# Experts in a new order: gathers of 256 slots, an early ranking, and biases of thin sets in one product

## The chip, the cores and the metric

One NeuronCore of a Trainium2 chip runs the whole program. The metric is the device time of one execution in microseconds, as the median of several runs. The engines are TensorE (PE for products, PEld for the loads of their stationary side), VectorE (DVE), ScalarE (ACT), GpSimd (POOL) and SyncE (SP). SP issues the transfers of weights here.

## The reference

Two blocks act on 512 tokens of width 1024, in fp32. The first has a mixer and then a mixture of experts (MoE); the second has two attention layers. The change lies in the MoE:

```python
logits = xt @ router_w + router_b
top_vals, top_idx = lax.top_k(logits, 4)          # 32 experts, 4 for each token
gates = softmax(top_vals)
# for each expert e, for the tokens that chose it:
hu = xb @ w_up[e] + b_up[e]                       # 1024 -> 2048
g, lin = minimum(hu[:, :1024], 7), clip(hu[:, 1024:], -7, 7)
y = ((lin + 1) * g * sigmoid(1.702 * g)) @ w_down[e] + b_down[e]
# summed over a token's experts, each times its gate
```

## The kernel before, in words

**Ranks and sets.** The router counts the tokens of each expert, and `moe_order` ranks the experts by count, the largest first (expert 0 stays first). It works with a handful of products and small vector operations, and leaves `self.order` (the expert of each rank, which SP reads into a register to address weights), `self.perm` (a one-hot matrix), `self.selr` (selectors for bias rows) and ranked copies of slots and gates (`Rp`, `tokp`). Ranks 0 to 17 have a *wide* set of 128 slots, ranks 18 to 31 a *thin* set of 64; rank 1 has a wide and a thin set. A rank is a *unit*.

**Precision.** Wide sets work with fp32r products. Every operand is split into a high and a low part, and three products stand for one. `moe_split` splits a half piece of weights: ScalarE makes the high part, VectorE the low part, into four pairs of buffers (`wh`/`wl` three, `sph`/`spl` one). Thin sets work with fp32 products on the raw weights, in two column halves of the array at once (64 slots each), and need no split. A thin set's raw buffer is held until TensorE is done with it; a wide set's until VectorE has split it.

**Weights.** Each expert has twelve pieces of 1 MB: four for each half of the up product, four for the down product. `load_piece` puts them into six raw buffers in turn (two `w`, four `w2`), so SP can be six pieces ahead. SP issues them in the order of their use: next unit's first half, last unit's down product, this unit's second half.

**A unit's work on TensorE** (`moe`): first half of the up product (`expert_up(0)`), in the middle of which the last unit's result is transposed (`mid`); then the last unit's down product (`moe_down`), whose rows GpSimd scatters into the residual in DRAM by an indirect transfer; in the last unit of a group, the gather of the next group; then the second half (`expert_up(1)`). The scheduler of the framework may move instructions of different strands past each other.

**Gathers.** `slot_sets` gathers the tokens of a *group* of units. It makes a one-hot matrix (`eoh`) on VectorE and multiplies: 8 chunks x 4 token tiles x 2 parts, 64 products, with as many columns as the group has slots. ScalarE takes the result from four banks of PSUM into `xT` (wide, split) or `xN` (thin). `moe_groups` writes the groups by hand: `[W]`, then pairs `[W T]` of 192 slots, rank 1 alone (192), one group `[W W]` of 256, more pairs: 17 groups.

**Biases.** `ebias` holds the bias rows of all experts, high and low parts. The last product of a group adds the expert's row: for a wide set one fp32r product of 512 columns with a selector column (`sel`), for a thin set two fp32 products, one for each column half (L1290, two records each).

Of the kernel before, what the change touches and what calls it, by code (L numbers as in the profile page):

```python
# [20 lines left out]
P = 128  # L21
# [41 lines left out]
for _n, _w in (("ident", 128), ("ones", 128), ("cmask", 128), ("smask", 128), ("cmpm", 4 * 32), ("cmpv", 4),  # L63
               ("invf", 32), ("hm", 4), ("hh", 2), ("lt", 128), ("gmask", 128), ("iota1", 128), ("iotap", 1),
               ("rst", S), ("lte", 128), ("selc", 32), ("lom", 1), ("dump", 1), ("ndd", 1), ("dn2", 1),
               ("keyb", 32), ("keyp", 1), ("cap", 1), ("avg", 4 * 64)):
    CST.add(_n, _w)
# [19 lines left out]
class Kern:  # L87
# [1006 lines left out]

    def moe_order(self):

# [6 lines left out]
        nc.tensor.matmul(ps[:, 0:NE], self.C["ones"], cnt.rearrange("p a e -> p (a e)"), start=True, stop=True)  # L1103
        nc.tensor.matmul(ps[:, NE:NE + 1], n4.rearrange("p a e -> p (a e)"), self.C["ones"][:, 0:1], start=True, stop=True)
        kb, self.perm = (self.t([P, NE], tag=f"ord{n}", bufs=1) for n in range(2))
        cc, kp, rank = (self.t([P, 1], tag=f"orc{n}", bufs=1) for n in range(3))
# [4 lines left out]
        nc.vector.tensor_reduce(rank, kb, axis=AXX, op=OP.add)  # L1111
        nc.vector.tensor_scalar(self.perm, self.C["iota1"][:, 0:NE], rank, None, op0=OP.is_equal)
        pe = self.perm[0:NE]
        ps = self.psum("tr")
        nc.tensor.matmul(ps[0:1, 0:NE], self.C["iotap"][0:NE], pe, start=True, stop=True)
        nc.tensor.matmul(ps[0:NE, NE:NE + 1], pe, cc[0:NE], start=True, stop=True)
        nc.tensor.matmul(ps[0:NE, NE + 1:NE + 2], pe, self.C["iotap"][0:NE], start=True, stop=True)
        self.order = self.t([1, NE], I32, tag="ori", bufs=1)
        nc.vector.tensor_copy(self.order, ps[0:1, 0:NE])

        self.cco = self.t([NE, 2], tag="cco", bufs=1)
        nc.vector.tensor_copy(self.cco, ps[0:NE, NE:NE + 2])
        for half in range(2):
            nc.gpsimd.tensor_scalar(self.selr[:, half, 1:NE], self.perm[:, 1:NE], self.C["hh"][:, half:half + 1], None,
                                    op0=OP.mult)
        bd = self.t([P, NT, NE], tag="orb", bufs=1)
        nc.vector.tensor_tensor(bd, self.perm[:, None, :].to_broadcast([P, NT, NE]),
# [4 lines left out]
        for n, v in enumerate(src):  # L1132
            nc.tensor.transpose(pt[:, n * P:(n + 1) * P], flat(v), self.ident)
        xt = self.t([P, 3 * P], tag="ort", bufs=1)
        nc.scalar.copy(xt, pt[:, 0:3 * P])
# [31 lines left out]

    def slot_sets(self, sets):


        nc = self.nc
        n = sum(self.width(kind) for kind, *_ in sets)
        oh = self.t([P, NT, 2 * C], F32R, tag="eoh", bufs=1)[:, :, 0:n]
        xs, at, o = [], [], 0
        for kind, R, *_ in sets:
            w = self.width(kind)
            sh = [P, NT, w]
            nc.vector.tensor_tensor(oh[:, :, o:o + w], self.C["iota1"][:, None, 0:w].to_broadcast(sh),
                                    R[:, :, None].to_broadcast(sh), op=OP.is_equal)
            if kind == "wide":  # L1180
                xs.append(self.t([P, 2, KC, C], F32R, tag="xT", bufs=2))
            else:
                xs.append(self.t([P, KC, CN], tag="xN", bufs=2))
            at.append(slice(o, o + w))
            o += w
        for k0, bank in zip(range(0, KC, 2), ("tr", "tr", "o", "o2")):
            pt = self.psum(bank)
            for q in range(2):
                k = k0 + q
                for t in range(NT):  # L1190
                    for m, r in enumerate(self.rows):
                        nc.tensor.matmul(pt[:, q * n:(q + 1) * n], r[:, t, k * P:(k + 1) * P], oh[:, t],  # L1192
                                         start=(t == m == 0), stop=(t == NT - 1 and m == 1))
            for (kind, *_), x, a in zip(sets, xs, at):
                f = self.t([P, 2, C], tag="ef", bufs=2) if kind == "wide" else x[:, k0:k0 + 2, :]
                for q in range(2):
                    k = k0 + q
                    nc.scalar.activation(f[:, q], pt[:, q * n + a.start:q * n + a.stop], AF.Identity,
                                         scale=self.s2[:, k:k + 1], bias=self.b2[:, k:k + 1])
                if kind == "wide":  # L1200
                    hi, lo = (x[:, m, k0:k0 + 2, :] for m in range(2))
                    nc.scalar.activation(hi, f, AF.Copy)
                    nc.vector.tensor_tensor(lo, f, hi, op=OP.subtract)
# [64 lines left out]
    def expert_mm(self, xT, pieces, ps, bias=None, ready=()):  # L1268

        nc = self.nc  # L1270
        xh, xl = xT
        for m, half in enumerate(self.half_pieces(pieces)):
            wh, wl = ready[m] if m < len(ready) else self.moe_split(*half)
            for q in range(2):
# [3 lines left out]
                nc.tensor.matmul(ps, xh[:, k, :], wl[:, q, :], start=False, stop=(k == KC - 1 and not bias))  # L1278
        if bias:
            nc.tensor.matmul(ps, *bias, start=False, stop=True)  # L1280

    def thin_mm(self, x, pieces, ps, bias=None):


        nc = self.nc
        ws = [(n, w.rearrange("p (k f) -> p k f", k=4)) for n, w in pieces]
        jobs = [(x[:, 4 * (n % 2) + q, :], w[:, q, :]) for n, w in ws for q in range(4)] + ([bias] if bias else [])
        for n, (a, w) in enumerate(jobs):
            for c in range(2):
                nc.tensor.matmul(ps[CN * c:CN * (c + 1), 0:256], a, w[:, c * 256:(c + 1) * 256], start=(n == 0),  # L1290
                                 stop=(n == len(jobs) - 1))

    def expert_up(self, half, sets, pieces, pos, mid=None, selr=None):
# [3 lines left out]
        selr = self.selr if selr is None else selr  # L1297
        sel = selr[:, half, pos:pos + 1]
        out = []
        for m, bank in enumerate(("mm", "s")):  # L1300
            row = self.ebias[:, m * 512:(m + 1) * 512]
            two = pieces[2 * m:2 * m + 2]

            for kind, x, _ in sorted(sets, key=lambda v: v[0]):
                ps = self.psum(bank)
                out.append((kind, ps))
                if kind == "wide":
                    self.expert_mm([x[:, n] for n in range(2)], two, ps, (sel.to_broadcast([P, P]), row))
                else:
                    self.thin_mm(x, two, ps, (sel.bitcast(F32).to_broadcast([P, CN]), row.bitcast(F32)))  # L1310
            if mid and not m:
# [65 lines left out]
    def moe_bias(self):  # L1377
# [5 lines left out]
        for m in range(4):  # L1383
            c0 = m // 2 * D
            nc.sync.dma_start(raw[32 * m:32 * m + 32], self.A["exp_b"][:, c0:c0 + D])
        yield
# [3 lines left out]
    @staticmethod  # L1390
    def moe_groups():


        wide = lambda n: (n, [("wide", 0)])
        thin = lambda n: (n, [("thin", 0)])
        pairs = [[wide(n + 2), thin(NF + n)] for n in range(NE - NF)]
        rest = [wide(n) for n in range(NE - NF + 2, NF)]
        rest = [rest[n:n + 2] for n in range(0, len(rest), 2)]
        both = [[(1, [("wide", 0), ("thin", C)])]]
        return [[wide(0)]] + pairs[:3] + both + pairs[3:6] + rest + pairs[6:]  # L1400

    def moe(self, xin):
# [11 lines left out]

        def make(g, R, tok):

            sets = []
            for pos, kinds in g:
                for kind, first in kinds:
# [5 lines left out]
                    sets.append((kind, r, tok[:, :, pos, :], dsts[:, n:n + 1], gates[:, n:n + 1]))  # L1425
            xs, index = self.slot_sets(sets)
            xs = iter(xs)
# [8 lines left out]
        for half in range(2):  # L1436
            nc.gpsimd.tensor_scalar(self.selr[:, half, 0:1], self.C["selc"][:, 0:1], self.C["hh"][:, half:half + 1], None,
                                    op0=OP.mult)
        self.g2n = self.t([P, 512], tag="g2n", bufs=1)
        for half in range(2):  # L1440
            r = slice(64 * half, 64 * half + 64)
            nc.gpsimd.tensor_copy(self.g2n[r], self.g2b[r, 512 * half:512 * half + 512])
        w = load(0, range(4))
        xs, index = make(groups[0], self.R, self.tok)
        index()
# [4 lines left out]
        for n, (pos, kinds) in enumerate(units):  # L1450
# [7 lines left out]
            if not n:  # L1458
                self.moe_order()
            if prev:  # L1460
# [54 lines left out]
    def job(self, selr):  # L1515
# [25 lines left out]
        for half in range(2):  # L1541
            nc.vector.tensor_tensor(selr[:, half], s1, self.C["hh"][:, half:half + 1], op=OP.mult)
        m = self.t([P, NT, NE], tag="orb", bufs=1)
        sel3 = selb[:, None, :].to_broadcast([P, NT, NE])
# [667 lines left out]
def const_array():  # L2212
# [35 lines left out]
    put("keyp", key[p % NE][:, None])  # L2248
    put("cap", np.array(CAP, np.float32)[p % NE][:, None])
    put("hh", np.where(p[:, None] // 64 == np.arange(2)[None, :], 1.0, 0.0))  # L2250
    put("hm", np.where(p[:, None] // 32 == np.arange(4)[None, :], 1.0, 0.0))
# [77 lines left out]
```

## Time and profile before

| | us |
|---|---|
| median of 3 runs | 2686.78 (2685.45 to 2688.61) |
| profiled execution | 2686.94 |
| its span, first to last instruction | 2685.1 |
| TensorE busy with products | 2561.9 (95%) |
| VectorE busy | 1796.4 (67%) |
| ScalarE busy | 1275.6 (48%) |
| MB moved, mean GB/s | 566.77, 211 |

The mixer takes the first 395 us, the MoE stands from there to about 1580 us, and the second block fills the rest. Starts of TensorE's products are read from the timeline; their ends are modelled, so the price of a product is read from start to start.

### The profile page before, as it was taken

Reading aid. Unit: us, or ns where it says so; the run is one execution under the profiler, and the core shown is the slowest. Engines: PE = TensorE matmul, PEld = TensorE weight load, DVE = VectorE, ACT = ScalarE, POOL = GpSimd, SP = SyncE. Lnnn points to the kernel's source line nnn. Section 1 sums busy time; section 2 is a strip of 40 time slices with the busy share of each in tenths; the row PEclk is TensorE's granted clock in tenths of the full one; section 3 lists DMA queues with packets and bytes.
Section 4 is the critical chain, followed back from the end, with each engine's and each line's share of the span. In section 5 each row is a group of like instructions: output and inputs, shape, how many; then the busy total and the mean of one; then the engine's idle time right before and its main releaser. Section 6 shows DMA issues by size and latency. Waiting matters only on the chain.

```text
span 2685.1 us, 40235 instructions
## 1 busy us (share of the span) xinstructions
PE 2561.9 (95%) x15431; PEld 2003.9 (75%) x15431; DVE 1796.4 (67%) x3400; ACT 1275.6 (48%) x2202; POOL 159.9 (6%) x151
## 2 busy tenths in 40 slices
PE   5998879999999999999999969989999999999998
PEld 5875678777777778777777757776777887767778
DVE  6886667666666688666666645596775656877764
ACT  3443546545555566444455534444444433534443
POOL 1001010100000000000000010011001000100001
PEclk9998788999999999999999989999999999999999
DMA  7531236999699999999999952221112521311124
GB/s 283 203 120 65 77 134 254 367 376 367 228 359 376 380 363 344 383 379 376 380 376 384 378 192 79 67 93 66 46 48 79 189 95 49 111 63 48 33 84 151
DMA packets 85828, 566.77 MB, mean 211 GB/s; under 512 B 9984, under 2 KB 10576, under 8 KB 22144
## 3 DMA queue, kind: packets, MB, share of 16 engines
q1 hardware_dynamic: 76368, 536.55, 51.5%
q0 software_dynamic: 7968, 24.16, 3.9%
q10 hardware_dynamic: 1296, 3.44, 0.3%
q8 instruction: 123, 2.02, 0.3%
q14 instruction: 73, 0.60, 0.1%
HBM read 543.93 MB, written 20.19 MB: 210 GB/s over the span
## 4 chain that ended last, share of the span: by engine, by line
PE 72%; DVE 6%; DMA 2%; ACT 2%; issue 2%; POOL 1%; ACTq 0%; DVEq 0%; SPq 0%; POOLq 0%
PE mm L396 5%; PE mm L397 5%; PE mm L398 5%; PE mm L1290 4%; PE s L1290 4%; PE o L1290 4%; PE o L1278 3%; PE mm L1276 3%; PE mm L1278 2%; PE o L1276 2%; PE o L1277 2%; PE s L1276 2%; PE mm L1277 2%; PE s L1278 2%; PE s L1277 2%; PE o L1192 2%
## 5 line engine op out<-in xcount | busy, mean ns | idle before, releaser
L1260 ACT ACTIVATE wh<-w 128x1024 fp32r<-128x1024 f32 x324 | 337.5, 1060 | 286.2 <-DMA w<-w_exp 131.7
L1261 DVE TENSOR_TENSOR wl<-w,wh 128x1024 fp32r<-128x1024 f32 x324 | 388.2, 1221 | 84.8 <-ACT wh L1260 84.0
L215 DVE TENSOR_TENSOR wl<-w,wh 128x1024 fp32r<-128x1024 f32 x194 | 237.0, 1223 | 176.3 <-ACT wh L214 175.1
L214 ACT ACTIVATE wh<-w 128x1024 fp32r<-128x1024 f32 x194 | 204.8, 1059 | 234.6 <-PE mm L397 97.9
L372 PE MATMUL mm<-wl,aTh 128*128 128x256 f32 x816 | 238.1, 293 | 5.6 <-DVE wl L215 5.6
L371 PE MATMUL mm<-wh,aTh 128*128 128x256 f32 x816 | 238.7, 294 | 2.2 <-ACT wh L214 1.3
L373 PE MATMUL mm<-wh,aTl 128*128 128x256 f32 x816 | 238.1, 293 | 0.8 <-DVE aTl L309 0.8
L396 PE MATMUL mm<-aTh,wh 128*128 128x512 f32 x560 | 228.3, 408 | 0.0
L397 PE MATMUL mm<-aTl,wh 128*128 128x512 f32 x560 | 225.5, 403 | 0.0
L398 PE MATMUL mm<-aTh,wl 128*128 128x512 f32 x560 | 224.9, 402 | 0.0
L372 PEld LDWEIGHTS mm<-wl,aTh 128*128 128x128 f32 x816 | 161.0, 197 | 9.4 <-DVE wl L215 6.3
L371 PEld LDWEIGHTS mm<-wh,aTh 128*128 128x128 f32 x816 | 160.4, 197 | 6.6 <-ACT wh L214 1.9
L373 PEld LDWEIGHTS mm<-wh,aTl 128*128 128x128 f32 x816 | 160.7, 197 | 4.5 <-issue 3.1
L464 ACT ACTIVATE P<-s,smx 128x256 f32<-128x256 f32 (+3 forms) x176 | 92.7, 528 | 86.8 <-DVE smx L461 85.7
L1261 DVE TENSOR_TENSOR spl<-w,sph 128x1024 fp32r<-128x1024 f32 x108 | 132.1, 1223 | 1.2 <-ACT sph L1260 1.2
L1260 ACT ACTIVATE sph<-w 128x1024 fp32r<-128x1024 f32 x108 | 114.2, 1057 | 26.5 <-PE mm L1277 10.3
L396 PEld LDWEIGHTS mm<-aTh,wh 128*128 128x128 f32 x560 | 106.3, 190 | 24.1 <-issue 4.9
L398 PEld LDWEIGHTS mm<-aTh,wl 128*128 128x128 f32 x560 | 106.3, 190 | 23.8 <-issue 3.0
L397 PEld LDWEIGHTS mm<-aTl,wh 128*128 128x128 f32 x560 | 105.8, 189 | 23.2 <-issue 3.8
L1319 DVE TENSOR_SCALAR eg<-s 128x512 f32<-128x512 f32 (+1 forms) x66 | 37.6, 569 | 111.6 <-PE s L1280 71.6
L1290 PE MATMUL mm<-w,xN 128*64 128x256 f32 x960 | 110.2, 382 | 0.0
L1290 PE MATMUL s<-w,xN 128*64 128x256 f32 x960 | 109.5, 381 | 0.0
(617 smaller groups left out, 6073.7 us busy)
## 6 DMA issues: line engine op xcount, KB each, us to landing
w<-w_exp SPq DMA_DIRECT2D x384, 1024.0 KB, 8.9
w<-w_in SPq DMA_DIRECT2D x57, 1024.0 KB, 4.8
w<-w_out SPq DMA_DIRECT2D x24, 1024.0 KB, 4.9
w<-ada_w SPq DMA_DIRECT2D x19, 1024.0 KB, 4.9
w<-cmp_w SPq DMA_DIRECT2D x8, 1024.0 KB, 4.8
w<-w_up SPq DMA_DIRECT2D x16, 512.0 KB, 3.3
xm<-hd POOLq DMA_DIRECT2D x5, 512.0 KB, 3.6
aTl<-ada_w SPq DMA_DIRECT2D x2, 1024.0 KB, 7.8
```

Source lines behind the costliest of these rows:

```text
L214: self.nc.scalar.activation(hi, src, AF.Copy)
L215: (self.nc.gpsimd if pool else self.nc.vector).tensor_tensor(lo, src, hi, op=OP.subtract)
L371: nc.tensor.matmul(v[:, q, :], ah[k][:, ts], w_h, start=(k == 0), stop=False)
L372: nc.tensor.matmul(v[:, q, :], ah[k][:, ts], w_l, start=False, stop=False)
L373: nc.tensor.matmul(v[:, q, :], al[k][:, ts], w_h, start=False, stop=(k == kk - 1))
L396: nc.tensor.matmul(ps, w_h, ah[k], start=(k == 0), stop=False)
L397: nc.tensor.matmul(ps, w_h, al[k], start=False, stop=False)
L398: nc.tensor.matmul(ps, w_l, ah[k], start=False, stop=(k == kk - 1))
L1260: nc.scalar.activation(hi, w, AF.Copy)
L1261: (nc.gpsimd if n in self.LO_POOL else nc.vector).tensor_tensor(lo, w, hi, op=OP.subtract)
L1276: nc.tensor.matmul(ps, xh[:, k, :], wh[:, q, :], start=(k == 0), stop=False)
L1290: nc.tensor.matmul(ps[CN * c:CN * (c + 1), 0:256], a, w[:, c * 256:(c + 1) * 256], start=(n == 0), stop=(n == len(jobs) - 1))
```

## The change

The groups have up to 256 slots: `[W T T]` or `[W W]` in a row written out by hand, 14 groups in place of 17; the thin ranks are taken from the smallest up. `moe_order` becomes a generator, `order_ranks`, which is run in steps from inside the first gather; its rest runs where the whole stood before. A thin set's bias is added by one fp32r product over the whole array, first in its group of products, with a selector matrix `selt` that GpSimd makes for each thin set; `ebias` is laid out for it, so that a wide set adds its bias in two products of 256 columns. A third buffer for `xN`, a constant `hcol` and two shared tags come with it.

```diff
-    def moe_order(self):
+    def order_ranks(self):
...
         nc.tensor.matmul(ps[:, NE:NE + 1], n4.rearrange("p a e -> p (a e)"), self.C["ones"][:, 0:1], start=True, stop=True)
+        yield
...
         nc.vector.tensor_scalar(self.perm, self.C["iota1"][:, 0:NE], rank, None, op0=OP.is_equal)
+        yield
         pe = self.perm[0:NE]
-        ps = self.psum("tr")
+        ps = self.psum("s")
...
         nc.vector.tensor_copy(self.order, ps[0:1, 0:NE])
+        yield
...
+        self.sele = self.perm
...
-    def slot_sets(self, sets):
+    def slot_sets(self, sets, mid=iter(())):
         nc = self.nc
+        next(mid, None)
...
-                xs.append(self.t([P, KC, CN], tag="xN", bufs=2))
+                xs.append(self.t([P, KC, CN], tag="xN", bufs=3))
...
+        next(mid, None)
         for k0, bank in zip(range(0, KC, 2), ("tr", "tr", "o", "o2")):
...
+            if k0 == 2:
+                next(mid, None)
...
-        if bias:
-            nc.tensor.matmul(ps, *bias, start=False, stop=True)
+        for c in range(2 if bias else 0):
+            nc.tensor.matmul(ps[:, c * 256:(c + 1) * 256], bias[0][:, c:c + 1].to_broadcast([P, P]), bias[1], start=False,
+                             stop=(c == 1))
...
-        jobs = [(x[:, 4 * (n % 2) + q, :], w[:, q, :]) for n, w in ws for q in range(4)] + ([bias] if bias else [])
+        if bias:
+            nc.tensor.matmul(ps[:, 0:256], *bias, start=True, stop=False)
+        jobs = [(x[:, 4 * (n % 2) + q, :], w[:, q, :]) for n, w in ws for q in range(4)]
...
+        if any(kind == "thin" for kind, *_ in sets) and not half:
+            self.selt = self.t([P, P], F32R, tag="selt", bufs=2)
+            nc.gpsimd.tensor_scalar(self.selt, self.hcol, self.sele[:, pos:pos + 1], None, op0=OP.mult)
...
-            c0 = m // 2 * D
-            nc.sync.dma_start(raw[32 * m:32 * m + 32], self.A["exp_b"][:, c0:c0 + D])
+            src = self.A["exp_b"][:, 0:2 * D].rearrange("e (g c j) -> e g c j", g=4, c=2)[:, :, m // 2]
+            nc.sync.dma_start(raw[32 * m:32 * m + 32].rearrange("p (g j) -> p g j", g=4), src)
...
-        pairs = [[wide(n + 2), thin(NF + n)] for n in range(NE - NF)]
-        rest = [wide(n) for n in range(NE - NF + 2, NF)]
-        rest = [rest[n:n + 2] for n in range(0, len(rest), 2)]
-        both = [[(1, [("wide", 0), ("thin", C)])]]
-        return [[wide(0)]] + pairs[:3] + both + pairs[3:6] + rest + pairs[6:]
+        w = [wide(n) for n in range(2, NF)][::-1]
+        t = [(n, [("thin", 0)]) for n in range(NF, NE)]
+        both = (1, [("wide", 0), ("thin", C)])
+        sizes = "3232313232313"
+        out = [[wide(0)]]
+        for n, c in enumerate(sizes):
+            if c == "3":
+                out.append([w.pop(), t.pop(), t.pop()])
+            elif c == "2":
+                out.append([w.pop(), w.pop()])
+            else:
+                out.append([both if n < 6 else w.pop()])
+        return out
...
+        nc.gpsimd.dma_start(self.hcol, self.A["cst"][:, o:o + n])
...
-        xs, index = make(groups[0], self.R, self.tok)
+        order = self.order_ranks()
+        xs, index = make(groups[0], self.R, self.tok, order)
...
             if not n:
-                self.moe_order()
+                for _ in order:
+                    pass
```

## Rows read from the trace of the kernel before

**Rows 1.** The page's span in 40 equal slices, busy tenths: TensorE, transfers.

```profile
PE   5998879999999999999999969989999999999998
...
DMA  7531236999699999999999952221112521311124
```

**Rows 2.** Stage windows: length, busy us of each engine, granted clock, DMA share, GB/s.

```profile
413.00:1557.00 1144.00, 1134.41 (x7281) 869.51 (x7280) 755.17 (x1015) 606.98 (x886) 68.98 (x34) 1.00 0.92 357
...
1170.06:1238.70 68.64, 68.04 (x455) 51.91 (x453) 43.24 (x58) 34.50 (x53) 3.84 (x2) 1.00 0.96 376
...
1238.70:1250.52 11.82, 11.82 (x53) 9.32 (x51) 8.63 (x9) 5.41 (x6) 2.29 (x1) 1.00 0.99 373
...
1219.36:1231.64 12.28, 12.28 (x59) 9.72 (x55) 7.56 (x14) 5.42 (x7) 0.00 (x0) 1.00 1.01 424
...
952.99:1045.47 92.48, 91.36 (x444) 74.15 (x442) 83.63 (x94) 66.11 (x81) 6.86 (x3) 1.00 0.94 350
...
420.00:440.00 20.00, 20.00 (x103) 16.41 (x102) 18.75 (x38) 11.16 (x13) 1.75 (x2) 1.00 0.26 100
```

**Rows 3.** Waits of TensorE's products, 390 to 1580 us: total us, times, longest.

```profile
PE o L1278 <- DVE wl L1261: 5.5, 10, 0.6
PE tr L1192 <- DVE vc L1499: 4.9, 1, 4.9
```

**Rows 4.** Transfer queue of the scatters, 1170 to 1239 us: packets, MB, share.

```profile
q0 software_dynamic: 288, 0.79, 6.0%
```

**Rows 5.** Chain that ended last: start, us, engine and line.

```profile
398.64 7.06 PE tr L1192 x32
...
1231.71 7.06 PE o L1290 x64
```

**Rows 6.** Stage windows of the gather products (L1192) alone: PE, PEld, clock.

```profile
398.64:1557.49 1158.85, 139.89 (x1088) 137.27 (x1088) 0.99 0.92 357
...
919.80:923.20 3.40, 3.40 (x29) 3.29 (x28) 1.00 0.93 325
1206.73:1210.29 3.56, 3.56 (x34) 3.51 (x32) 1.00 1.02 350
...
398.64:412.33 13.69, 13.69 (x64) 13.69 (x64) 0.50 0.96 368
```

**Rows 7.** Timeline of TensorE: start, us, line, out<-in, shape, records.

```profile
1210.34 3.67 PE L1290 MATMUL mm<-w,xN 128*64 128x256 f32 x32
1213.85 0.60 PE L1290 MATMUL mm<-ebias,selr 128*64 128x256 f32 x4
1214.28 3.62 PE L1290 MATMUL s<-w,xN 128*64 128x256 f32 x32
1217.73 0.60 PE L1290 MATMUL s<-ebias,selr 128*64 128x256 f32 x4
1218.26 0.61 PE L1217 MATMUL tr<-orT,eoh 128*128 128x4 f32 x4
...
1250.20 0.39 PE L1280 MATMUL s<-ebias,selr 128*128 128x512 f32 x1
1250.52 0.44 PE L1290 MATMUL mm<-w,xN 128*64 128x256 f32 x2
```

**Rows 8.** Weight loads (L209), 1170 to 1239 us: from issue to landing.

```profile
DMA to landing us min/median/max: 4.7/9.4/13.1
```

**Rows 9.** Waits of TensorE's products, 925 to 965 us.

```profile
PE mm L1278 <- DVE wl L1261: 1.6, 2, 1.1
```

**Rows 10.** Waits of SP, 400 to 440 us.

```profile
SPq L209 <- DVE orc L1111: 29.9, 1, 29.9
```

**Rows 11.** Timeline of GpSimd, 395 to 600 us.

```profile
401.15 0.29 POOL L1101 COPY rn<-before 128x128 f32<-128x128 f32 x1
...
433.76 1.75 POOL L1124 TENSOR_SCALAR selr<-ord,cstcmask 128x31 fp32r<-128x31 f32 x2 [31.96 <-DVE ord L1112]
...
576.15 1.55 POOL L1374 DMA_INDIRECT xm<-ey,eix  x1 [32.58 <-DVE ey L1366]
```

More of the change, by code (lines that the diff above doesn't have):

```diff
@@ L65 @@
                ("rst", S), ("lte", 128), ("selc", 32), ("lom", 1), ("dump", 1), ("ndd", 1), ("dn2", 1),
-               ("keyb", 32), ("keyp", 1), ("cap", 1), ("avg", 4 * 64)):
+               ("keyb", 32), ("keyp", 1), ("cap", 1), ("avg", 4 * 64), ("hcol", 128)):
     CST.add(_n, _w)
@@ L1125, in moe_order @@
                                     op0=OP.mult)
-        bd = self.t([P, NT, NE], tag="orb", bufs=1)
+        bd = self.t([P, NT, NE], tag="eg1", bufs=1)
         nc.vector.tensor_tensor(bd, self.perm[:, None, :].to_broadcast([P, NT, NE]),
@@ L1133, in moe_order @@
             nc.tensor.transpose(pt[:, n * P:(n + 1) * P], flat(v), self.ident)
-        xt = self.t([P, 3 * P], tag="ort", bufs=1)
+        xt = self.t([P, 3 * P], tag="eg0", bufs=1)
         nc.scalar.copy(xt, pt[:, 0:3 * P])
@@ L1286, in thin_mm @@
         ws = [(n, w.rearrange("p (k f) -> p k f", k=4)) for n, w in pieces]
-        jobs = [(x[:, 4 * (n % 2) + q, :], w[:, q, :]) for n, w in ws for q in range(4)] + ([bias] if bias else [])
+        if bias:
+            nc.tensor.matmul(ps[:, 0:256], *bias, start=True, stop=False)
+        jobs = [(x[:, 4 * (n % 2) + q, :], w[:, q, :]) for n, w in ws for q in range(4)]
         for n, (a, w) in enumerate(jobs):
             for c in range(2):
-                nc.tensor.matmul(ps[CN * c:CN * (c + 1), 0:256], a, w[:, c * 256:(c + 1) * 256], start=(n == 0),
+                nc.tensor.matmul(ps[CN * c:CN * (c + 1), 0:256], a, w[:, c * 256:(c + 1) * 256], start=(n == 0 and not bias),
                                  stop=(n == len(jobs) - 1))
@@ L1297, in expert_up @@
         selr = self.selr if selr is None else selr
-        sel = selr[:, half, pos:pos + 1]
+        sel = selr[:, :, pos]
+        if any(kind == "thin" for kind, *_ in sets) and not half:
+            self.selt = self.t([P, P], F32R, tag="selt", bufs=2)
+            nc.gpsimd.tensor_scalar(self.selt, self.hcol, self.sele[:, pos:pos + 1], None, op0=OP.mult)
         out = []
         for m, bank in enumerate(("mm", "s")):
-            row = self.ebias[:, m * 512:(m + 1) * 512]
+            row = self.ebias[:, (2 * half + m) * 256:(2 * half + m + 1) * 256]
             two = pieces[2 * m:2 * m + 2]
@@ L1307, in expert_up @@
                 if kind == "wide":
-                    self.expert_mm([x[:, n] for n in range(2)], two, ps, (sel.to_broadcast([P, P]), row))
+                    self.expert_mm([x[:, n] for n in range(2)], two, ps, (sel, row))
                 else:
-                    self.thin_mm(x, two, ps, (sel.bitcast(F32).to_broadcast([P, CN]), row.bitcast(F32)))
+                    self.thin_mm(x, two, ps, (self.selt, row))
             if mid and not m:
@@ L1394, in moe_groups @@
         wide = lambda n: (n, [("wide", 0)])
-        thin = lambda n: (n, [("thin", 0)])
-        pairs = [[wide(n + 2), thin(NF + n)] for n in range(NE - NF)]
-        rest = [wide(n) for n in range(NE - NF + 2, NF)]
-        rest = [rest[n:n + 2] for n in range(0, len(rest), 2)]
-        both = [[(1, [("wide", 0), ("thin", C)])]]
-        return [[wide(0)]] + pairs[:3] + both + pairs[3:6] + rest + pairs[6:]
+        w = [wide(n) for n in range(2, NF)][::-1]
[11 more added lines that the diff above has]
+        return out
     def moe(self, xin):
@@ L1413, in moe, with make @@
         cols = {}
-        def make(g, R, tok):
+        def make(g, R, tok, mid=iter(())):
             sets = []
@@ L1425, in make @@
                     sets.append((kind, r, tok[:, :, pos, :], dsts[:, n:n + 1], gates[:, n:n + 1]))
-            xs, index = self.slot_sets(sets)
+            xs, index = self.slot_sets(sets, mid)
             xs = iter(xs)
@@ L1438, in moe @@
                                     op0=OP.mult)
+        self.hcol = self.t([P, P], tag="hcol", bufs=1)
+        o, n = CST.at["hcol"]
+        nc.gpsimd.dma_start(self.hcol, self.A["cst"][:, o:o + n])
         self.g2n = self.t([P, 512], tag="g2n", bufs=1)
@@ L1542, in job @@
             nc.vector.tensor_tensor(selr[:, half], s1, self.C["hh"][:, half:half + 1], op=OP.mult)
-        m = self.t([P, NT, NE], tag="orb", bufs=1)
+        m = self.t([P, NT, NE], tag="eg1", bufs=1)
         sel3 = selb[:, None, :].to_broadcast([P, NT, NE])
@@ L2249, in const_array @@
     put("cap", np.array(CAP, np.float32)[p % NE][:, None])
+    put("hcol", np.where(p[:, None] // 64 == np.arange(P)[None, :] // 64, 1.0, 0.0))
     put("hh", np.where(p[:, None] // 64 == np.arange(2)[None, :], 1.0, 0.0))
```

## The prediction

> **What bounds the kernel now.** I read the page's forty slices first. In slices 7 to 22, the expert phase, TensorE is busy nine tenths or more, and the transfers are nearly as full [rows 1]. Two resources compete there, so the next question is which of them the other waits for.
>
> The stage windows say TensorE. From 413 to 1557 us it is busy 1134.41 of 1144.00 us at the full clock, and one steady pair of a wide and a thin unit takes 68.64 us with 68.04 busy [rows 2]. The waits agree: over the whole phase the products wait 5.5 us in total for the split's low part and 4.9 us once at the first gather, and nothing else is longer [rows 3]. So time taken off TensorE in this phase comes off the end, as long as the weights keep arriving.
>
> They have little to spare. In a full stretch the queue moves 424 GB/s, so a piece of 1.0486 MB takes 2.48 us [rows 2]. A pair needs 24 pieces, 59.5 us, and its two scatters take 6.0% of the engines for about the pair's time, 4.1 us (wide 2.7, thin 1.4, by their sizes): 63.6 us of transfers against 68.64 us of TensorE [rows 2, 4]. The margin is 5 us a pair on average, and an average hides the order. A half of a wide unit gives TensorE 11.82 us for four pieces, which is 9.9 us of transfers; the down product of a thin unit gives 7.06 us for the same four [rows 2, 5]. Wide units refill the six raw buffers, thin units drain them.
>
> **Gathers.** Before there are 17: one of 128 slots, 15 of 192, one of 256, each 64 products whatever the width. After there are 14: two of 128, one of 192, eleven of 256. The columns in sum stay the same, so everything hangs on what a product costs by width. 29 products of 256 columns fill 3.40 us, 0.117 us each; of 192 columns 32 start in 3.56 us, 0.111 each; the first gather's 64 of 128 take 13.69 us at a granted clock of 0.50 (1.2 GHz), 0.214 each, hence 0.107 at twice that [rows 6]. The width is almost free. At those spacings the late gathers cost 15 x 7.10 + 7.49 = 114.0 us before and 11 x 7.49 + 7.10 + 6.85 = 96.3 after: 17.7 saved. All gathers together are busy 139.89 us [rows 6], so with their interruptions the 16 late ones average (139.89 - 13.69) / 16 = 7.9 us; if the interruptions go too, the saving nears 21. I take 19, with 17.7 and 21 as ends.
>
> **Thin biases.** A thin set has four bias steps, each of four records (two fp32 products, one for each column half). Starts give the price. The step at 1213.85 takes 0.43 us when thin products follow; the one at 1217.73 takes 0.53 when work 128 wide follows [rows 7]. Leaving the thin shape costs 0.10. Entering it costs 0.08: a wide bias ahead of thin work takes 0.32 us [rows 7], one of the 50 products that fill a wide half 11.82 / 50 = 0.24 [rows 2]. Before, a set pays 3 x 0.53 + 0.43 + 3 x 0.08 = 2.26 us. After, each step is one fp32r product of 256 columns on the whole array; the nearest row is the gather's, 0.117 [rows 6]. But it stands inside thin work, so every block goes from 128 wide to thin and back: 0.12 + 0.08 + 0.10 = 0.30, 1.2 us a set. Saved 1.06 a set, 16 us for 15 sets. Bounds: with no price for shapes 2.02 - 0.48 = 1.54 a set, 23 us; if the new product costs as much as a thin step with both changes (0.61), nothing. It has the gather product's shape, so nothing is too low an end; I keep 5 and 23.
>
> The Trainium skill, TensorEngine Tiling (Array Packing), Key Properties, says that changing the tiling mode drains the array, and gives no figure. The 0.43 against 0.53 us agrees. Without a drain this edit would be worth 23 us, with it 16.
>
> **Wide biases.** One product of 512 columns becomes two of 256: 2 x 0.117 against 0.24 [rows 2, 6]. I cost it at nothing.
>
> **Weights for two thin units in a row.** The new order is W, WTT, WW, WTT, WW, WTT, the unit with both kinds, WTT, WW, WTT, WW, WTT, W, WTT. Seven times two thin units stand together; before they never did. From the start of the first thin unit to the end of its down product TensorE needs 2 x (3.51 + 0.30) = 7.6, a wide down product of 11.3 (the 11.82 half without its biases), 7.6, 7.6 for the second unit's first half, and 7.06: 41.2 us [rows 2, 5, 7]. Those 20 pieces take 49.6 us and a wide scatter 2.7: 52.3. The shortage is 11 us. What can cover it is five raw buffers ahead, 12.4 us, less what a landing takes beyond its own 2.48 us (the shortest landing is 4.7): 10.2 [rows 8]. So each double thin stands on the edge. I take 1 us for each, 7 in all; ends 0 and 21. The one after the unit with both kinds has a single wide unit ahead instead of three: 2 us more. The last has no gather behind it: its remaining 7.6 + 7.06 = 14.7 us meet 8 pieces and a scatter, 21.2 us: 6 us. Together 15.
>
> **Gathers of two wide sets.** Before there is one, at 904 to 923 us, and TensorE then waits 1.6 us for low splits [rows 9]. After there are four: 3 us more (0 to 9). A run of three wide units, of which there are five after, occurs once before, at 953 to 1045 us: VectorE is busy 83.63 of 92.48 us there, TensorE 91.36 [rows 2]. The run itself costs nothing.
>
> **Ranking.** Now SP waits 29.9 us for the ranking before it loads for the second unit [rows 10], and the queue falls to 100 GB/s in 420 to 440 us [rows 2]. Moved into the first gather, that wait goes. But TensorE is busy all 20.00 of these 20 us: the first unit's eight landed pieces hide the wait, so its end is worth nothing, and the ranking's products are the same. What it may cost is at the first gather. The counts need a copy that GpSimd starts at 401.15 us [rows 11], behind the copies of the gate row and now behind one more transfer issue, while the gather starts at 398.64 [rows 5]. If the counts stand ahead of the gather in TensorE's order, it starts 3 us late. I take 1.5 (0 to 4). The bias rows, now fetched in runs of 1 KB, and the new mask are wanted 20 and 80 us after their issue, which hides them.
>
> **GpSimd.** For each thin set it makes a 128x128 mask. The nearest row makes two of 128x31 in 1.75 us, so one takes 0.9 to 3.6. It queues behind a scatter that waits 32.58 us for its rows [rows 11]. For the second thin unit that scatter is the wide unit's, whose rows are ready when the first thin unit's second half begins; 7.6 us remain, and a wide scatter (1.55) and the mask fit. Nothing, then; if late, TensorE stands at the bias, which now opens the block.
>
> **The sum.** The profiled execution took 2686.94 us (span 2685.1, 1.8 around it), 0.2 above the median of 2686.78. Saved 19 + 16 = 35; given back 15 + 3 + 1.5 = 19.5; net 15.5: 2671 us.
>
> **Rivals.**
> *Weights keep up.* The double thins cost nothing and only the end loses 6: -35 + 6 + 1.5, 2659 us. For it: no wait for weights is among TensorE's long ones before [rows 3]. Against: 41.2 us of work for 52.3 of transfers.
>
> *Weights bind.* Each double thin loses 3 us: 21 + 2 + 6 + 4.5 = 33.5 given back, 2685 us, no change to be measured. For it: the 10.2 us assume buffers that are all full. Against: gathers and runs of wide units refill them.
>
> The Trainium skill, DMA: Bandwidth & Descriptors, Specifications, would put this rival first: it limits a core's reads from HBM to about 358 GB/s. By that a pair's 25.2 MB take 70.3 us, more than TensorE's 68.64, and the change saves nothing, 2687. The trace disagrees: 424 GB/s over 12 us, 376 over the pair [rows 2].
>
> *VectorE becomes the bound.* In the five runs of three wide units, with wider evacuations around them, the low splits fall behind; VectorE is already 90% busy in such a run [rows 2]. At 7 us a run, 35 replace my 3: 2703 us, slower. It decides from about 4 us a run on. Against: the one run before lost next to nothing.
>
> *The bias edit is worth little,* 5 us and not 16, which also leaves the weights more time (12 and not 15): -24 + 12 + 4.5, 2679 us.
>
> **Chances.** Forecast 0.50, weights keep up 0.22, weights bind 0.12, VectorE 0.08, biases 0.08. The likeliest gives 2671 us, alone 2661 to 2681. The range for 8 in 10 goes down past the second case, with the upper ends of gathers and biases (-44 + 6: 2649), and up to no change, 2687. What a measurement here can tell from no change is about 0.2%, 5.4 us: faster 0.76, within 0.14, slower 0.10.
>
> **What would show it.** Right: 896 gather products and not 1088, thin bias blocks 0.3 us long, waits of TensorE for weights at the down product of each first thin unit and at the end, 15 us in all, and a first gather near its old start. Wrong: those waits absent or tripled, long waits for low splits in the runs of wide units, a bias that waits for GpSimd, 256-column gather products well above 0.117 us.

## The result, and the profile after

The changed kernel takes 2703.9 us (median of four runs, 2699.35 to 2707.42) against 2686.1 before: ratio 1.0065, 95% interval 1.0047 to 1.0082. It is slower by 18 us where 15.5 us faster was forecast, and lies above the range. The profiled execution took 2699.35 us with a span of 2697.6, 12.5 us above that of before.

The page's slices, TensorE and transfers, answer to [rows 1]. Below them stand the stage windows (columns as in [rows 2]) of the expert phase, of a stretch around two thin units in a row (a *double thin*), and of its middle:

```profile
PE   5998879999999999999999969999999999999998
...
DMA  7531146998999979999899952131112521211124
```

```profile
413.00:1571.00 1158.00, 1121.51 (x6975) 842.98 (x6975) 748.88 (x998) 606.97 (x886) 102.89 (x45) 1.00 0.93 352
640.00:760.00 120.00, 114.42 (x729) 83.15 (x729) 72.56 (x99) 54.76 (x78) 15.77 (x6) 1.00 0.99 381
700.00:720.00 20.00, 17.75 (x150) 12.06 (x149) 4.57 (x15) 2.96 (x8) 0.97 (x1) 1.00 1.01 423
```

TensorE has less to do than before (1121.5 us busy against 1134.4) in a longer phase: it stands idle for 36.5 us, where it stood for 9.6 [rows 2]. The tenths hide this. In the double thin stretch the transfers are full (0.99 to 1.01) and TensorE is not (0.95, then 0.89). What it waits for, by the wait view, 390 to 1590 us:

```profile
PE tr L1345 <- DVE eat L1337: 10.5, 11, 1.1
PE mm L1288 <- DVE wl L1270: 6.5, 10, 1.1
PE o L1199 <- DVE eyn L1387: 5.4, 9, 0.7
PE tr L1199 <- DVE vc L1528: 4.9, 1, 4.9
PE s L1303 <- DMA w<-w_exp: 2.5, 3, 1.6
PE o L1288 <- DVE wl L1270: 2.4, 5, 0.5
PE o L1286 <- ACT wh L1269: 2.2, 5, 0.5
PE tr L1105 <- POOL rn L1102: 2.0, 1, 2.0
```

Before, the same view has for the transposes of thin results:

```profile
PE tr L1329 <- DVE eat L1321: 2.1, 2, 1.1
```

New against [rows 3] are gathers that wait for an evacuation (eyn). Transposes that wait for a thin unit's swiglu (eat) grew from 2.1 to 10.5 us, products that wait for low splits (wl, spl) from 7.3 to 10.5. Weights (w_exp) are a small entry, 4.5 us in all. The list speaks against late weights; the experiments show that it misleads. The timeline of TensorE in one double thin shows the same, and something else:

```profile
691.39 1.95 PE L1303 MATMUL s<-w,xN 128*64 128x256 f32 x16
693.26 0.39 PE L1199 MATMUL tr<-eoh,aTh 128*128 128x256 f32 x1
...
694.87 1.95 PE L1303 MATMUL s<-w,xN 128*64 128x256 f32 x16
696.75 0.38 PE L1199 MATMUL tr<-eoh,aTh 128*128 128x256 f32 x1
...
702.81 3.62 PE L1303 MATMUL s<-w,xN 128*64 128x256 f32 x32
707.51 0.41 PE L1345 MATMUL tr<-cstident,eat 128*128 128x128 f32 x2 [1.08 <-DVE eat L1337]
707.85 3.67 PE L1303 MATMUL o<-w,ean 128*64 128x256 f32 x32
712.11 0.39 PE L1199 MATMUL o<-eoh,aTh 128*128 128x256 f32 x1 [0.59 <-DVE eyn L1387]
```

The gather is cut into pieces inside thin blocks, and the transposes stand right behind the products whose result they need, not behind the next unit's first products as in the source. The framework wrote another order. By the timelines, a thin result's transposes follow directly on the second block of a thin half in 2 places before and in 10 after; changes between gather products and thin work (products or biases) went from 25 to 96.

Of the parts, the gathers' busy time (windows of their line alone) answers to [rows 6]:

```profile
394.70:1578.00 1183.30, 130.86 (x896) 119.78 (x896) 0.99 0.92 350
```

896 products as forecast, but 130.86 us, where the same gathers take 113.87 if they aren't cut (in the run with the order held, below). SP's longest wait for the ranking [rows 10] fell from 29.9 to 5.8 us. TensorE waits once, for 2.0 us, for the counts. The first gather starts at 394.70 in place of 398.64, but it starts anywhere from 393.1 to 398.9 in these runs, with the new ranking or the old.

Summed from start to start over the phase (first gather to last thin product, 1165.6 us before, 1183.4 after), biases of thin sets went down by 16.4 us and gathers by 14.8; products of thin sets rose by 36.0 and those of wide sets by 16.2. So the gains were there, and the products around them gave back more.

### The profile page after: what moved, and what is told of

Read it like the earlier page. It is cut to its first block, busy times and chain, and to the rows that moved or that the text cites. A ratio compares the mean times of both kernels' runs of the same rounds, so it can differ in the third digit from the quotient of the medians.

```text
span 2697.6 us, 39710 instructions
## 1 busy us (share of the span) xinstructions
PE 2545.3 (94%) x15131; PEld 1975.5 (73%) x15131; DVE 1792.4 (66%) x3400; ACT 1275.6 (47%) x2202; POOL 196.0 (7%) x167
## 4 chain that ended last, share of the span: by engine, by line
PE 71%; DVE 8%; ACT 2%; issue 2%; DMA 2%; POOL 1%; ACTq 0%; DVEq 0%; POOLq 0%
PE mm L396 5%; PE mm L397 5%; PE mm L398 5%; PE mm L1303 4%; PE s L1303 4%; PE o L1303 3%; PE mm L1288 3%; PE o L1288 3%; PE s L1286 2%; PE s L1288 2%; PE o L1286 2%; PE s L1287 2%; PE o L1287 2%; PE mm L1286 2%; PE mm L1287 2%; PE s L443 2%
## 5 line engine op out<-in xcount | busy, mean ns | idle before, releaser
L1303 PE MATMUL o<-w,ean 128*64 128x256 f32 x960 | 113.3, 384 | 2.1 <-DMA w<-w_exp 1.0
```

## The experiments

Ratios are to the kernel before, with 95% intervals.

**The parts alone.** The groups, the biases and the ranking, each put alone into the kernel before, and the change with another order inside its groups of three:

```diff
 a1 (kernel before): moe_groups of the change, and
-                xs.append(self.t([P, KC, CN], tag="xN", bufs=2))
+                xs.append(self.t([P, KC, CN], tag="xN", bufs=3))
 a2 (kernel before): moe_bias, expert_mm, thin_mm, selt and hcol of the change
 a3 (kernel before): order_ranks, run from inside the first gather
 a4 (changed kernel):
-                out.append([w.pop(), t.pop(), t.pop()])
+                out.append([t.pop(), w.pop(), t.pop()])
```

> The kernel before with the new order of units and the third buffer for thin tokens alone; biases and ranking stay old. Theory (two thin units in a row and runs of three wide ones cost TensorE more than the gathers save: the products of thin sets took 36 us more after the change, those of wide sets 16 us more, the gathers 15 us less): slower than before by 25 to 45 us, and slower than the changed kernel by about the 16 us of the biases. Rival (the new order is harmless, and the loss comes from the new biases or the early ranking): 10 to 20 us faster than before.

2713.3 us, 1.0102 (1.0085 to 1.0118): the groups alone lose 27 us, as the theory said. They stand 9 us above the changed kernel and not 16, for the biases are worth less (next run).

> The kernel before with the new biases alone (one fp32r product first in each thin block, two of 256 columns for a wide set, and the mask of GpSimd). Both the prediction and the theory: about 16 us faster, 2670 us (12 to 19). Rival (each bias inside thin work costs TensorE its pipeline, or waits for the mask): within 5 us of before, or slower.

2682.0 us, 0.9977 (0.9967 to 0.9987): 4 us gained by the medians, 6 by the ratio, not 16. The timeline of a steady thin half in this run:

```profile
1205.42 0.30 PE L1291 MATMUL mm<-ebias,selt 128*128 128x256 f32 x1
1205.66 3.67 PE L1295 MATMUL mm<-w,xN 128*64 128x256 f32 x32
1209.26 0.39 PE L1291 MATMUL s<-ebias,selt 128*128 128x256 f32 x1
1209.58 3.67 PE L1295 MATMUL s<-w,xN 128*64 128x256 f32 x32
1213.18 0.61 PE L1218 MATMUL tr<-orT,eoh 128*128 128x4 f32 x4
```

The step between two thin blocks takes 0.32 us, start to start, and each block 3.60 where it took 3.51 and 3.45 [rows 7]: the way out of the thin shape is paid by the block's last product. 0.42 in all there, where 0.30 was forecast; behind a gather it is 0.24 and 0.10.

> The kernel before with the ranking run in steps from inside the first gather, nothing else. Theory: within 4 us of before, since eight landed pieces hid SP's wait. Rival (the ranking delays the first gather, and everything stands behind it): 3 to 6 us slower. Other rival (the weights were behind for long after the ranking): 5 us or more faster.

2688.0 us, 1.0010 (1.0001 to 1.0020): about the 1.5 us of the prediction, and no gain.

> The changed kernel with each group of three ordered thin, wide, thin, so that no two thin units follow each other and at most two wide units do; same gathers of 256 slots, same biases, same ranking. Theory (the neighbours' order costs the time): the thin sets' extra 36 us and most of the wide sets' 16 go, 2650 to 2668 us, 20 to 36 us faster than before. Rival (256-slot gathers between thin and wide work, or their evacuations, cost it): stays near 2700 us. Rival (weights bind on the average, and what is saved on TensorE is only waited for): near 2686 us.

2690.1 us, 1.0013 (1.0004 to 1.0023): 14 us better than the changed kernel, but short of what I expected, and nearest to the last rival (weights bind). Waits for swiglu (10.5 us) were as large as in the changed kernel and those for splits larger (12.8 at the first block, where it had 6.5), though no two thin units were neighbours. My theory of neighbours' chains fell here.

**Bytes and order.** Half the bytes, in both kernels, and the order held by hand. The edits are written short: `piece` stands for the whole expression of the address, and the hand-over of pieces that are already split (`ready`) is left out:

```diff
 b1 (changed kernel), b0 (kernel before):
-            w = self.load_piece(piece)
+            w = self.load_piece(piece[:, 0:1024])     # and each half of a piece reads these
 b2 (changed kernel), b4 (a4):
             if mid and not m:
-                mid()
+                with self.behind(self.pe):            # PE order: behind the last product so far
+                    mid()
...
-                more, index = make(groups[g], self.Rp, self.tokp)
+                with self.behind(self.pe):
+                    more, index = make(groups[g], self.Rp, self.tokp)
-            self.expert_up(1, sets, wu, pos)
+            with self.behind(self.pe):
+                self.expert_up(1, sets, wu, pos, ahead=ahead if early else None)
 # ahead: load the next wide unit's first pieces, split four halves, then the swiglu's last steps
```

> The changed kernel with weights of half the bytes: of each expert piece only the first half is loaded and stands for the second half too, so the experts' results are other ones; all products, splits and their number stay. The framework then also writes another order: transposes behind the next unit's first products, splits of the next wide unit ahead of the thin unit's swiglu, gathers in one stretch. Theory (the order of the instructions on each engine, written as if weights came later than they do, costs the time): 2650 to 2670 us, 30 to 50 us below the changed kernel. Rival (two thin units in a row lose the time by the length of their own chain from products to swiglu to transposes): stays above 2690 us. The rival that weights bind expects the same fall, and is told apart by the two next kernels.

2649.7 us, 0.9864 (0.9848 to 0.9880), 54 us below the changed kernel.

> The kernel before with weights of half the bytes in the same way (the experts' results are other ones). Theory: TensorE hardly waited for weights before, so at most 10 us come back, 2676 to 2687 us. Rival (transfers are the second bound before as well): 25 us or more.

2682.3 us, 0.9979 (0.9966 to 0.9991): 4 us. Bytes cost the kernel before almost nothing and the changed one 54 us. But in b1 the order changed as well (transposes behind a thin half's second block in 1 place and not 10, changes between gather and thin work 15 and not 96), so it frees two things at once. The order of b0 isn't quite that of before either: transposes of wide results wait 6.7 us for their swiglu there, a wait that the list of before doesn't have. So the 4 us may be some 7 too few.

> The changed kernel, all bytes of the weights, with the order held by hand: transposes of the last unit behind the first products of the next, a gather behind the down product, the second half of the up product behind the gather, and the splits of a wide unit's first four half pieces ahead of the last step of the swiglu of the thin unit before it. Theory (order): as with half the bytes, 2650 to 2675 us. Rival (weights bind, and the order only filled the gaps): 2690 us or more, with TensorE waiting for weights in the double thin units in place of the transposes. Rival (the length of the chain): near 2700 us.

2704.9 us, 1.0070 (1.0053 to 1.0087): nothing gained, as the rival said. Its waits (390 to 1590 us), and the timeline of the double thin shown above:

```profile
PE o L1303 <- DMA w<-w_exp: 14.4, 26, 0.8
PE s L1303 <- DMA w<-w_exp: 5.2, 9, 1.4
PE mm L1288 <- DVE wl L1270: 5.0, 5, 1.0
PE o L1288 <- DVE wl L1270: 4.9, 8, 0.7
```

```profile
698.62 1.95 PE L1303 MATMUL s<-w,xN 128*64 128x256 f32 x16
701.07 1.95 PE L1303 MATMUL s<-w,xN 128*64 128x256 f32 x16 [0.50 <-DMA w<-w_exp]
703.65 1.95 PE L1303 MATMUL o<-w,ean 128*64 128x256 f32 x16 [0.64 <-DMA w<-w_exp]
706.16 1.95 PE L1303 MATMUL o<-w,ean 128*64 128x256 f32 x16 [0.56 <-DMA w<-w_exp]
708.63 1.95 PE L1303 MATMUL o<-w,ean 128*64 128x256 f32 x16 [0.53 <-DMA w<-w_exp]
711.02 1.95 PE L1303 MATMUL o<-w,ean 128*64 128x256 f32 x16 [0.44 <-DMA w<-w_exp]
```

With the transposes and the gather out of the way, TensorE waits for weights openly: each piece of the first thin unit's down product comes some 2.5 us after the one before, and 16 products take 1.95. The wait list of the changed kernel had named what the framework put into this gap. The sign that the prediction gave, waits for weights at a first thin unit's down product, was in the right place and shows only now. In all, the list names weights with 20 us and splits, which need landed weights too, with 15.

> The order thin, wide, thin in each group of three, and the same holds on the order of instructions. Theory: the 14 us that the order of units alone gave back and the waits that were left (32 us in the phase) fall together, 2650 to 2670 us. Rival (weights bind): within 8 us of the order of units alone, 2690 us.

2696.1 us, 1.0027 (1.0012 to 1.0042): no gain either, 6 us above the order of units alone, as the rival said.

**Depth of the buffers.** Five, six or seven raw buffers (seven cost the fourth pair of split buffers):

```diff
-            with self.phase("moe", NW2=4, NP=1):
+            with self.phase("moe", NW2=5, NP=1):     # c1, c4 with NSP = 0;  c2, c3: NW2=3
```

> The changed kernel with seven raw buffers in place of six (five of w2), paid for with the fourth pair of split buffers (sph and spl go). Theory (each double thin unit runs out of landed weights, and the six buffers can't carry over what arrives too early in the runs of wide units): a piece more ahead, 2.5 us for each of seven double thin units, 15 to 25 us faster than the changed kernel, 2680 to 2690 us, less what the missing split pair costs (0 to 10). Rival (the order of the instructions or the chain through the swiglu costs the time): no gain, 2700 us or more.

2705.2 us, 1.0066 (1.0050 to 1.0083): no gain, as the rival said, though the missing split pair may hide a small one (in the kernel before, at the end of this section, the same exchange costs 3 us).

> The changed kernel with five raw buffers in place of six. Theory: 2.5 us more for each of seven double thin units and some at the wide units behind them, 20 to 35 us slower than the changed kernel, 2722 to 2740 us. Rival (order or chain): within 8 us of the changed kernel.

2709.9 us, 1.0093 (1.0076 to 1.0111): 6 us lost, far less than expected and within the rival's 8.

> The kernel before with five raw buffers. Theory: alternate wide and thin units drain the buffers by 2.8 us at a thin down product and fill them at once, so with one piece less ahead 0 to 15 us are lost, less than in the changed kernel: 2686 to 2701 us. Rival (the depth matters alike everywhere): 20 us or more.

2728.6 us, 1.0160 (1.0143 to 1.0177): 42 us lost, the opposite of what I expected. But the framework wrote another order here too: changes between gather and thin work went from 25 to 55, and gathers and transposes take 16 us more from start to start. What the missing buffer costs in an unchanged order, no run shows. The changed kernel, which keeps its order nearly as it was with five buffers, loses 6.

> The order thin, wide, thin with seven raw buffers and three pairs of split buffers. Theory: what this order still loses to late weights around its two thin units comes back, 10 to 20 us below 2690, 2670 to 2680 us, which would be below the kernel before. Rival (its loss lies in the splits): 2690 us or more, since a split pair is missing.

2686.8 us, 0.9997 (0.9987 to 1.0006): 3 us below the same order with six buffers, and between theory and rival.

**Both at once.** The order held with seven buffers, and with half the bytes:

```diff
 d1 (b2):  NW2=5, NSP = 0, and
-                ready.extend(self.moe_split(*v) for v in self.half_pieces(w[:2]))
+                ready.extend(self.moe_split(*v) for v in self.half_pieces(w[:2])[:3])
 d2 (b2):
-            w = self.load_piece(piece)
+            w = self.load_piece(piece[:, 0:1024])
```

> The changed kernel with the order held by hand and seven raw buffers, three pairs of split buffers (three half pieces split ahead, not four). One buffer more gave nothing to the order as the framework wrote it, and the order held by hand gave nothing with six buffers. Theory (both limits stand at about the same place, so each alone hides the other): together they give 10 to 25 us, 2680 to 2695 us. Rival (the rate of the transfers is the bound over the whole stretch, so depth is worth nothing): 2700 us or more. Rival (the missing split pair costs more than the buffer gives): above 2705 us.

2692.0 us, 1.0021 (1.0012 to 1.0031): 13 us below the order held with six buffers. Each alone had given nothing.

> The order held by hand and half the bytes of the weights (the first half of each piece stands for the second too, so the experts' results are other ones); TensorE's order is the same as in the run with the order held and all bytes, but for three places. Theory (in that order TensorE waits for weights and for little else): 45 to 55 us below it, 2650 to 2660 us. Rival (its loss is the length of the chains, which bytes don't change): 2690 us or more.

2648.7 us, 0.9865 (0.9849 to 0.9882): 56 us below nearly the same order with all bytes (by the timelines more than three places differ, but by small moves: groups of a few products, transposes and index products stand somewhat earlier or later). The first lines of its waits have no weights and no swiglu left, and in the stretch of the double thin TensorE is busy all 20 us:

```profile
PE tr L294 <- DVE w L260: 17.6, 1, 17.6
PE tr L1199 <- DVE vc L1544: 4.8, 1, 4.8
PE o L1286 <- ACT wh L1269: 2.7, 6, 0.5
```

```profile
700.00:720.00 20.00, 20.00 (x159) 15.92 (x156) 9.56 (x18) 13.47 (x31) 2.88 (x2) 1.00 0.65 203
```

(The 17.6 us stand in the second block; before, they are 16.6, which [rows 3] leaves out.) One period of five units, W T T W W, from the first product of a thin unit (rank 29) to that of rank 27, read from the timelines:

| kernel | two thin units, to rank 6 | three wide ones, to rank 27 | period |
|---|---|---|---|
| changed | 64.8 | 115.4 | 180.2 |
| changed, five buffers | 64.8 | 115.4 | 180.2 |
| changed, seven buffers | 64.4 | 115.8 | 180.2 |
| order held | 62.3 | 117.8 | 180.0 |
| order held, seven buffers | 60.4 | 117.0 | 177.4 |
| order held, half the bytes | 58.8 | 112.5 | 171.3 |

As built, the period is 180.2 us whatever the buffers, so I put it down to the order. That is argued and not shown: no run has the built order with fewer bytes, for the framework rewrites it. With the order held the period is 180.0, and bytes and buffers move it: the weights set it. So it looks as if two limits stand at the same place, and taking away either shows only the other.

With the order held, the stage windows (columns as in [rows 2]) of the two thin units with the first half of the wide one behind them, and of the other two wide units:

```profile
666.90:749.00 82.10, 79.44 (x580) 56.85 (x579) 38.30 (x62) 32.24 (x55) 4.34 (x4) 1.00 1.02 400
762.35:846.95 84.60, 82.22 (x424) 66.42 (x422) 72.52 (x87) 59.17 (x81) 10.26 (x2) 1.00 0.86 323
```

The transfers are full over 82 us and at 0.86 over 85 later ones, 0.94 over the period. So the weights are late in one part while the queue has room in the other. Six buffers don't carry that room over, it seems: a seventh gives 2.6 us a period.

**A version that beats both.** The order thin, wide, thin with what was learnt, a hold more, and a control:

```diff
 d3 (b4): NW2=5, NSP = 0, three halves split ahead; gather and second half not held:
-                with self.behind(self.pe):
-                    more, index = make(groups[g], self.Rp, self.tokp)
+                more, index = make(groups[g], self.Rp, self.tokp)
 e1 (d3): a wide unit behind a thin one loads and splits ahead of the thin down product
+                    wu = load(pos, range(4, 8))
+                    ready = [self.moe_split(*v) for v in self.half_pieces(wu[:2])[:3]]
+                    hold = self.lo_ins
...
-                    nc.vector.scalar_tensor_tensor(y[:, fs], ps[:, 0:256], gate, ...)
+                    with self.behind(hold if half else None):
+                        nc.vector.scalar_tensor_tensor(y[:, fs], ps[:, 0:256], gate, ...)
 e2 (kernel before): NW2=5, NSP = 0
```

> The order thin, wide, thin with seven raw buffers and three split pairs, transposes held behind the next unit's first products and three half pieces split ahead of the thin unit's swiglu; gathers left free to fill gaps. Theory: the 26 us of waits that the run with seven buffers still had for the swiglu and the splits fall by half or more, 2665 to 2680 us, below the kernel before. Rival (the transfers set this order's pace too): 2682 us or more.

2680.6 us, 0.9982 (0.9973 to 0.9992): just above the theory's range and below the rival's.

> The last kernel (thin, wide, thin; seven raw buffers; transposes and splits held) with one hold more: where a wide unit follows a thin one, three half pieces of its second half are split ahead of the second evacuation of the thin unit's down product. Theory (VectorE does these splits behind an evacuation that waits 3 us for TensorE, though ScalarE has its part ready): some 12 waits of 1 us and the delay around them go, 8 to 16 us below that run, 2665 to 2673 us. Rival (the weights land too late for it): within 4 us of 2681.

2667.2 us, 0.9925 (0.9912 to 0.9937): 20 us faster than the kernel before and 37 faster than the change. VectorE in the run before this edit and in this one, at the same place of the program:

```profile
1077.70 0.48 DVE L1392 SCALAR_TENSOR_TENSOR eyn<-o,eix,g2n 128x256 f32<-128x256 f32 x1 [2.20 <-PE o L1303]
1081.15 0.48 DVE L1392 SCALAR_TENSOR_TENSOR eyn<-o,eix,g2n 128x256 f32<-128x256 f32 x1 [2.97 <-PE o L1303]
1081.55 5.98 DVE L1270 TENSOR_TENSOR wl<-w,wh 128x1024 fp32r<-128x1024 f32 x5
```

```profile
1072.47 0.48 DVE L1393 SCALAR_TENSOR_TENSOR eyn<-o,eix,g2n 128x256 f32<-128x256 f32 x1 [2.20 <-PE o L1303]
1072.87 3.49 DVE L1270 TENSOR_TENSOR wl<-w,wh 128x1024 fp32r<-128x1024 f32 x3
1076.27 0.48 DVE L1393 SCALAR_TENSOR_TENSOR eyn<-o,eix,g2n 128x256 f32<-128x256 f32 x1
```

The splits now fill the 2.97 us in which VectorE had waited for TensorE; of the 11.1 us of waits for them at the first blocks 0.4 are left in the list.

> The kernel before with seven raw buffers and three pairs of split buffers. Theory: it hardly waits for weights, so depth gives at most 4 us and the missing split pair takes at most 6: 2682 to 2692 us. Rival (the last kernels are faster than before by their buffers alone): 2678 us or less.

2690.5 us, 1.0011 (1.0000 to 1.0022): seven buffers alone don't make the kernel before faster.

## Why the prediction was wrong

*Gathers, right in kind, too small.* Forecast 19 us, 21 at most. With the order held the gathers' line is busy 113.87 us against 139.89 [rows 6], and from start to start they fall by 22.9; as built, cut up, by 14.8. The end of 21 was too low by its own rows: late gathers of 126.2 us with all their interruptions, 96.3 without any, leave room for 29.9. A product of 128 columns takes 0.112 us at the full clock (d2, 1375 us, clock 1.00), where I had 0.107 from half of its time at 0.50; over 64 products that is 0.3 us.

*Thin biases, mis-sized.* Forecast 16. From start to start the biases of thin sets and the thin products together fall by 7 us in a2 and by 11 with the order held and half the bytes (8 and 12 with the biases of wide sets). The new step costs up to 0.42 and not 0.30. The Trainium skill, TensorEngine Tiling (Array Packing), Key Properties, says that a change of tiling mode drains the array; the 0.10 us on the block's last product and the 0.20 on the bias agree, and my 0.30 counted the way out of the thin block, but too little on the way in.

*The sum of what is saved, right partly by luck.* 35 us forecast; with the weights out of the way the phase falls from 1165.6 to 1130.4 us, 35.2, and the time by 37, of which 4 are the half bytes' own. But gathers gave 4 us more than forecast, thin biases 5 fewer, and the transposes fell by 3 that I hadn't counted.

*Weights for two thin units in a row: the step that failed.* I let them give back 15 us: 1 us at each double thin, 2 more behind the unit with both kinds, 6 more at the end. Measured between all and half the bytes with the order held: 56 us, less the 4 to 11 that the kernel before pays, so 45 to 52. In the period shown, against half the bytes, the two thin units lose 3.5 us held and 6.0 as built, the wide run behind them 5.3 and 2.9, 8.8 and 8.9 in all, and I had given that run nothing. Two numbers were too kind. The price of a transfer: I added 2.48 us a piece, from the best 12 us, to the scatters, 63.6 us a pair, while the row of the pair itself says 0.96 of 68.64, 65.9 [rows 2]; over the double thin stretch the full queue moves 381 GB/s, 2.75 us a piece, and 20 pieces take 55 us, not 52.3 with the scatter. And the margin: I set the shortage against one stretch, but taking 35 us off TensorE takes 2.5 us off each pair, and of the margin of 2.7 that leaves nothing to refill the buffers with.

*That an order stays as written, not in the prediction at all.* With weights this short the framework wrote another order on TensorE and VectorE, which costs the same 180 us a period. I read program order as the chip's.

*Ranking, GpSimd, wide biases: as forecast,* nothing or 1 to 2 us.

*The rivals.* "Weights bind" was the right mechanism, but its 33.5 us (29 of them for the weights) were too small as well; its chance was 0.12. The Trainium skill, DMA: Bandwidth & Descriptors, Specifications, gives about 358 GB/s as a core's limit, half of what a stack of HBM gives two cores, which also says "no gain"; here one core runs the program, and 423 GB/s stand over 20 us and 381 over 120, so the limit isn't there, though the phase as a whole runs at 352. VectorE as the bound, which gave the number 2703, met the measured time by chance: VectorE is busy 749 of 1158 us, and with half the bytes it does the same work while its lateness is gone. "The bias edit is worth little, 5 us" held for the size of that edit, and not as the reason for the loss.

What stays open: how much of the loss, in the kernel as built, is the order's own, and why the written order's period equals that of the held one so closely. That the framework plans with a price of transfers near the real one would explain it; the built order turns clean when the bytes are halved, but its plan is in no trace.

## What to carry to other kernels

When a wait list after a change names many small waits for results and few for data, don't conclude that data were in time: hold the order and look again, for work moved into a gap hides the gap's owner. Test a suspected limit together with its rival limit, because two of equal size each show nothing when taken away alone. Look, too, whether an edit of buffers or bytes changed the order of the instructions, for then it tests two things. And when the second resource is at 0.96, take its need from share times length of the whole stretch, and count every microsecond saved on the first as lost from the margin.

## What the runs showed of the hardware

An fp32r product of 128 rows by 256 columns between two thin blocks costs 0.32 us from start to start and 0.10 on the product ahead, against 0.117 in a row of its like. And the queue moved 400 GB/s over 82 us at a share of 1.02, and 323 GB/s at 0.86 over 85 us later in the same period (order held): a mean of 0.94 hid a stretch in which it was full.
